# Layer 0 starts with v on unscaled, transposed tokens; v is computed ahead of q and k

## The chip, the cores and the metric

The kernel runs on one core of one Trainium2 chip. A core has TensorE (matrix products, PE in the rows), VectorE (DVE), ScalarE (ACT), GpSimd (POOL) and SyncE (SP), which issues most transfers; each takes its instructions strictly in the order of its own queue and meets the others through semaphores. The metric is the device time of one execution in microseconds (us); the median of three runs of the kernel before is 469.36 (469.34 to 469.58).

## The reference

Two layers of a decoder trunk on 256 tokens of 1024 channels, in float32. What matters here is the front of a layer, and which parts read which:

```
h = rms_norm(x, ln_w)                  # x * rsqrt(mean(x*x) + eps) * ln_w, per token
proj = h @ w_in                        # 1024 x 6672
q, k, v, g_attn, z, xbc, dt_raw = split(proj)
q, k = rms_norm per head (8 heads of 128) of q, k
attn = causal attention with ALiBi (q, k, v) * silu(g_attn)     # 256 tokens: one block
xbc  = silu(causal depthwise conv of width 4 (xbc)); xs, B, C = split(xbc)
dt   = softplus(dt_raw + dt_bias)
y    = SSD scan (xs, dt, a_log, B, C, d_skip) * silu(z), grouped rms_norm
x    = x + concat(attn, y) @ w_out
```

The norm's factor of a token is one number per row, so `(x * ln_w) @ w_v` times that factor, row by row, is the same v.

## The kernel before, in words

Every large product is made of float32r parts: an operand is split into a high part (a cast) and a low part (the operand less its high part), and three products, high-high, low-high and high-low, are added in PSUM. Weights come as a stream of pieces of two k tiles (128 x 2 x 512 numbers for most chunks, 128 x 2 x 348 or 344 for v): `load` (L72) issues the transfer on SyncE into one of four raw buffers, and `pump` (L82) casts the high part on ScalarE (L92) and subtracts for the low part (L94) on VectorE, on GpSimd for pieces 0 and 4. Eight split pieces are held at most, and `free` gives one back after its last product. The chunks go in the order of `CHUNKS` (L34): q0, k0, v0 to v2 (the last holds dt's columns too), q1, k1, and on.

`mm_tokens` (L196) makes q, k, v and the output, tokens on PSUM's partitions, for one half `t` of the 256 tokens over all pieces of a chunk: 24 products for 8 k tiles. q0 and k0 are made for the first 128 tokens and then for the others, while all their eight pieces are held. `mm_pair` (L216) makes x, B, C, g and z with channels on the partitions.

The tokens are loaded with tokens on the partitions. `pre_norm` (L238) normalizes 128 of them: ScalarE's sums of squares, a small "me" on VectorE (L243), the power of -1/2 on GpSimd (L169), the scaling into `hn`, eight transposes on TensorE into `tp`, the product with ln_w on VectorE into `hw`, a cast on ScalarE into `hT` and a subtract on VectorE into `lT`. At the start this runs for the first half ahead of the first product; the second half's runs a little later, its transposes among the products. Ten products of ones (`warm`, L149) stand first on TensorE.

The order on each engine is partly the order of the program, where `manual_schedule` says so (ScalarE, VectorE and TensorE at the start, TensorE at the end of a layer), and otherwise made by a scheduler when the kernel is built. Work behind a product (norms, attention heads, the scan) is written as generators that are resumed some pieces later: `tick` counts pieces, and a `yield n` asks for n more.

Of the kernel before, what the change touches and what calls it, by code (L numbers as in the profile page):

```python
# [9 lines left out]
F32 = mybir.dt.float32  # L10
# [5 lines left out]
P = 128  # L16
# [10 lines left out]
# columns of the per-partition parameters of a layer  # L27
# [21 lines left out]
class Weights:  # L49
    """The stream of weight pieces: loaded ahead, split into two float32r parts."""  # L50

    def __init__(self, nc, raw_pool, wh_pool, wl_pool, w):
# [3 lines left out]
        off = 0  # L56
# [57 lines left out]
def hybrid_kernel(ctx: ExitStack, tc: tile.TileContext, x, par, w, out):  # L114
# [60 lines left out]
    # Work that follows a product is traced a few pieces of weights later, so that the  # L175
    # tensor engine does not wait for it.
# [19 lines left out]
    def mm_tokens(L, name, t, lh, ll, ps, start, stop, last, cols=None):  # L196
# [3 lines left out]
        ts = slice(t * P, (t + 1) * P)  # L200
        cs = slice(*(cols or (0, wd)))
        for s in range(kt // KS):
            ws.pump()
            wh, wl = ws.parts[i0 + s]
            for kk in range(KS):
                kl = k0 % KT + s * KS + kk
                first = start and s == 0 and kk == 0
                final = stop and s * KS + kk == kt - 1
                pe.matmul(ps[:, cs], lh[:, kl, ts], wh[:, kk, cs], start=first, stop=False)  # L209
                pe.matmul(ps[:, cs], ll[:, kl, ts], wh[:, kk, cs], start=False, stop=False)  # L210
                pe.matmul(ps[:, cs], lh[:, kl, ts], wl[:, kk, cs], start=False, stop=final)  # L211
# [26 lines left out]
    def pre_norm(L, t, hT, lT, ms, wait, first=False):  # L238
        """RMS-norm of 128 tokens, split and with the channels on the partitions."""
# [26 lines left out]
        if first:  # L266
            yield 0
# [68 lines left out]
    def decay(L, dtr, dt, dth, ac, nac, cb):  # L336
        """dt = softplus, cumulative sums of dt * exp(a_log): per token and as rows for all."""
# [39 lines left out]
    def conv(L, ps, pr, dst):  # L377
        """Causal convolution and 2 * silu of the channel tiles 2 * pr, 2 * pr + 1."""
# [30 lines left out]
    def ssd_quarter(L, pr, x2, dth, ac, nac, cb, cm, dsh):  # L409
        """Decayed C B products and y of the heads 4 * pr .. 4 * pr + 3."""  # L410
# [83 lines left out]
    for t in range(2):  # L494
        msum[t] = small.tile([P, 2], F32, tag="ms", name=f"ms{t}")
    for j in range(2):
        square_sum(0, j, msum[0])
    for L in range(NL):
        pc = L * NPAR
        if L == 0:  # L500
            hT = keep.tile([P, KT, S], F32R, tag="hT", name=f"hT{L}")
            lT = keep.tile([P, KT, S], F32R, tag="lT", name=f"lT{L}")
            with tc.manual_schedule(engines={mybir.EngineType.Activation, mybir.EngineType.DVE,
                                             mybir.EngineType.PE}):
                start = pre_norm(L, 0, hT, lT, msum[0], 0, True)
                next(start)
                next(start)
                ws.pump(1)
                next(start, None)
                ws.pump(2)  # L510
            ws.pump(4)
            for j in range(2):
                square_sum(1, j, msum[1])
        resume(pre_norm(L, 1, hT, lT, msum[1], 7))

# [1 line left out]
        qT = keep.tile([P, NH, S], F32, tag="qT", name=f"qT{L}")  # L517
        kT = keep.tile([P, NH, S], F32, tag="kT", name=f"kT{L}")
        v_sb = keep.tile([P, 2, D], F32, tag="v", name=f"v{L}")
        aT = keep.tile([P, NH, S], F32, tag="aT", name=f"aT{L}")  # L520
# [7 lines left out]
        def qk(nm, c, t):  # L528
            ps = ps_p.tile([P, 512], F32, tag="ps_p", name=f"{nm}{c}{t}")
            mm_tokens(L, f"{nm}{c}", t, hT, lT, ps, True, True, t == 1)  # L530
            if nm == "q":
                resume(qk_post(L, ps, c, t, qT, C_QN, 1.0, P * EPS))
            else:
                resume(qk_post(L, ps, c, t, kT, C_KN, 1.0 / P, EPS))

        for t in range(2):
            qk("q", 0, t)
            qk("k", 0, t)
# [149 lines left out]
```

## Time and profile before

| | |
|---|---|
| median of three runs | 469.36 us |
| profiled execution, first to last instruction | 467.3 us (its time outside this span isn't recorded) |
| TensorE, VectorE, ScalarE, GpSimd busy | 458.6, 342.4, 278.3, 28.6 us |
| bytes read | 76.8 MB, 167 GB/s over the span |
| granted clock of TensorE, mean | 0.992 |

Times of rows count from the span's first instruction. A product's row is longer than its distance from the next one, since products are pipelined; distances of starts, or the chain of waits, give what one costs in a row.

### The profile page before, as it was taken

What the parts mean: (1) busy time and instruction counts of PE and PEld (TensorE: products, weight loads), DVE (VectorE), ACT (ScalarE), POOL (GpSimd) and SP (SyncE); (2) the same over time, 40 slices, a digit from 0 to 9 for tenths busy, and PEclk for the clock granted to TensorE, in tenths of its full rate; (3) what the DMA queues carried; (4) which work ended last, traced back from release to release, by engine and by line L of the source; (5) the groups of instructions that cost most, each with busy time, mean ns of one, the idle gap of its engine ahead of it and who ended that gap; (6) DMA issues with size and microseconds to landing.
All of it is one profiled execution on the core that took longest, in us unless ns stands there. A gap on an engine that the chain in (4) does not pass through costs nothing.

```text
span 467.3 us, 7748 instructions
## 1 busy us (share of the span) xinstructions
PE 458.6 (98%) x2912; PEld 409.1 (88%) x2912; DVE 342.4 (73%) x621; ACT 278.3 (60%) x563; POOL 28.6 (6%) x31
## 2 busy tenths in 40 slices
PE   5999999999999999999999999999999999999996
PEld 5789987899999898888788899879999989988885
DVE  5765577778999897787385557866899989876721
ACT  6667565987745853446365575678776655555400
POOL 3211001100000000100001100110000000010000
PEclk9799999999999999999999999999999999999999
DMA  7566775832536234536360768574443444434401
GB/s 282 200 193 178 243 271 182 320 131 93 189 130 211 89 118 166 180 129 225 96 194 19 216 212 286 187 299 149 163 156 116 150 165 137 146 103 158 135 24 67
DMA packets 25781, 78.38 MB, mean 168 GB/s; under 512 B 2544, under 2 KB 9104, under 8 KB 25232
## 3 DMA queue, kind: packets, MB, share of 16 engines
q1 hardware_dynamic: 25744, 77.89, 49.3%
q8 instruction: 23, 0.38, 0.3%
q14 instruction: 14, 0.11, 0.1%
HBM read 76.80 MB, written 1.08 MB: 167 GB/s over the span
## 4 chain that ended last, share of the span: by engine, by line
PE 96%; DMA 1%; DVE 1%; ACT 1%; SPq 0%; issue 0%; POOL 0%; DVEq 0%
PE o L210 6%; PE o L209 6%; PE o L211 6%; PE xb L227 5%; PE xb L228 5%; PE xb L229 5%; PE q L210 4%; PE z L229 3%; PE q L211 3%; PE z L228 3%; PE q L209 3%; PE z L227 3%; PE v L209 3%; PE v L211 3%; PE v L210 3%; PE g L228 3%
## 5 line engine op out<-in xcount | busy, mean ns | idle before, releaser
L94 DVE TENSOR_TENSOR wl<-raw,wh 128x1024 fp32r<-128x1024 f32 (+2 forms) x142 | 163.4, 1168 | 44.8 <-ACT wh L92 32.8
L92 ACT CAST wh<-raw 128x1024 fp32r<-128x1024 f32 (+2 forms) x144 | 143.0, 1003 | 63.4 <-PE o L210 21.4
L229 PE MATMUL xb<-hT,wl 128*128 128x256 f32 x192 | 54.8, 285 | 0.0
L228 PE MATMUL xb<-lT,wh 128*128 128x256 f32 x192 | 54.6, 285 | 0.0
L227 PE MATMUL xb<-hT,wh 128*128 128x256 f32 x192 | 54.5, 284 | 0.0
L228 PE MATMUL g<-lT,wh 128*128 128x256 f32 x128 | 36.5, 285 | 0.0
L228 PEld LDWEIGHTS xb<-lT,wh 128*128 128x128 f32 x192 | 36.2, 189 | 0.2
L227 PEld LDWEIGHTS xb<-hT,wh 128*128 128x128 f32 x192 | 36.2, 189 | 0.2
L229 PE MATMUL z<-hT,wl 128*128 128x256 f32 x128 | 36.4, 284 | 0.0
L229 PEld LDWEIGHTS xb<-hT,wl 128*128 128x128 f32 x192 | 36.2, 189 | 0.1
L227 PE MATMUL z<-hT,wh 128*128 128x256 f32 x128 | 36.3, 283 | 0.0
L229 PE MATMUL g<-hT,wl 128*128 128x256 f32 x128 | 36.2, 283 | 0.0
L228 PE MATMUL z<-lT,wh 128*128 128x256 f32 x128 | 36.2, 283 | 0.0
L227 PE MATMUL g<-hT,wh 128*128 128x256 f32 x128 | 36.0, 281 | 0.0
L393 DVE SCALAR_TENSOR_TENSOR cv<-rw,par_sb,cv 128x256 f32<-128x256 f32 x72 | 32.2, 483 | 4.0 <-ACT cv L390 4.0
L209 PE MATMUL v<-wh,hT 128*128 128x348 f32 (+1 forms) x96 | 30.9, 322 | 0.0
L210 PE MATMUL v<-wh,lT 128*128 128x348 f32 (+1 forms) x96 | 30.9, 322 | 0.0
L211 PE MATMUL v<-wl,hT 128*128 128x348 f32 (+1 forms) x96 | 30.8, 321 | 0.0
L209 PE MATMUL q<-wh,hT 128*128 128x512 f32 x64 | 27.2, 425 | 1.3 <-ACT hT L271 1.3
L210 PE MATMUL q<-wh,lT 128*128 128x512 f32 x64 | 26.6, 416 | 1.8 <-DVE lT L274 1.8
L211 PE MATMUL q<-wl,hT 128*128 128x512 f32 x64 | 26.3, 411 | 0.0
L209 PE MATMUL k<-wh,hT 128*128 128x512 f32 x64 | 25.7, 401 | 0.0
(164 smaller groups left out, 1092.3 us busy)
## 6 DMA issues: line engine op xcount, KB each, us to landing
raw<-in_w_dram SPq DMA_DIRECT2D x120, 512.0 KB, 4.3
raw<-in_w_dram SPq DMA_DIRECT2D x16, 348.0 KB, 3.9
cb<-cd SPq DMA_DIRECT2D x4, 1024.0 KB, 5.3
raw<-in_w_dram SPq DMA_DIRECT2D x8, 344.0 KB, 4.3
out_dram<-x SPq DMA_DIRECT2D x3, 256.0 KB, 2.1
x<-in_x_dram SPq DMA_DIRECT2D x2, 256.0 KB, 2.8
x<-in_x_dram SPq DMA_DIRECT2D x1, 512.0 KB, 6.8
out_dram<-x SPq DMA_DIRECT2D x2, 128.0 KB, 1.8
```

Of the source, the lines that this page charges most:

```text
L92: nc.scalar.copy(h[:, :, :wd], src)
L94: sub.tensor_tensor(lo[:, :, :wd], src, h[:, :, :wd].bitcast(F32), ALU.subtract)
L209: pe.matmul(ps[:, cs], lh[:, kl, ts], wh[:, kk, cs], start=first, stop=False)
L210: pe.matmul(ps[:, cs], ll[:, kl, ts], wh[:, kk, cs], start=False, stop=False)
L211: pe.matmul(ps[:, cs], lh[:, kl, ts], wl[:, kk, cs], start=False, stop=final)
L227: pe.matmul(o, wh[:, kk, cs], lh[:, k, :], start=(k == 0 and c == 0), stop=False)
L228: pe.matmul(o, wh[:, kk, cs], ll[:, k, :], start=False, stop=False)
L229: pe.matmul(o, wl[:, kk, cs], lh[:, k, :], start=False, stop=(k == KT - 1 and c == 1))
L393: dve.scalar_tensor_tensor(cv[:, c, :], rw[:, c, k:k + S], cw(k), cv[:, c, :], ALU.mult, ALU.add)
```

## The change

The host lays a transposed copy of x (128 partitions x 8 k tiles x 256 tokens) in front of the weights. It is loaded in four pieces of two k tiles, each ahead of a weight piece, into `xT`; the parameters are loaded from ScalarE's queue, and the row-laid x, in two halves, behind these. `CHUNKS` now begins with v0, v1, v2.

In layer 0, `first_tokens` multiplies a piece of `xT` by ln_w and splits it, without the norm, into `hr` (two casts with a scale on ScalarE) and `lr` (VectorE); v and dt are made of these, and the norm's factor `rs0` is applied when v leaves PSUM on ScalarE and when dt is read. `first_scale` makes `rs0` of the row-laid x. `first_norm` brings the factors to all partitions by two products of ones with a diagonal, multiplies `xT` by them and splits it into `hT` and `lT` for everything after v. The 16 transposes of layer 0 are gone. In layer 1 the norm is as before.

`mm_tokens` takes a list of halves and works each piece for all of them. q and k are made for both halves piece by piece, after v; v0 and v1 of layer 1 are made for the first half of the tokens and then for the second, v2 and all v of layer 0 for both halves piece by piece. The first four attention heads are due at 5, 9, 13 and 17 pieces instead of 1, 5, 9 and 13, counted from after k0.

```diff
-CHUNKS = [(n, 0, 8, 512) for n in ("q0", "k0")]
-CHUNKS += [("v%d" % i, 0, 8, V_W[i]) for i in range(3)]
-CHUNKS += [(n, 0, 8, 512) for n in ("q1", "k1", "x2", "x0", "x1", "g0", "g1", "z0", "z1")]
+CHUNKS = [("v%d" % i, 0, 8, V_W[i]) for i in range(3)]
+CHUNKS += [(n, 0, 8, 512) for n in ("q0", "k0", "q1", "k1", "x2", "x0", "x1", "g0", "g1", "z0", "z1")]
...
-    nc.sync.dma_start(x_sb[0][:, :512], x[0:P, :512])
-    nc.sync.dma_start(x_sb[0][:, 512:], x[0:P, 512:])
     par_sb = const.tile([P, NL * NPAR], F32, name="par_sb")
-    ws.load(0)
-    nc.sync.dma_start(par_sb, par)
-    ws.load(1)
-    nc.sync.dma_start(x_sb[1], x[P:2 * P, :])
+    nc.scalar.dma_start(par_sb, par)
+    xT = keep.tile([P, KT, S], F32, tag="aT", name="xT")
+    xsrc = w[0:NX].rearrange("(p k n) -> p k n", p=P, k=KT)
+    for s in range(KT // KS):
+        ks = slice(s * KS, (s + 1) * KS)
+        nc.sync.dma_start(xT[:, ks, :], xsrc[:, ks, :])
+        ws.load(s)
+    for t in range(2):
+        nc.sync.dma_start(x_sb[t], x[t * P:(t + 1) * P, :])
...
+            for t, ps in zip(ts, pss):
+                tl = slice(t * P, (t + 1) * P)
+                for kk in range(KS):
...
+    def first_tokens(s, hr, lr):
+        ks = slice(s * KS, (s + 1) * KS)
+        for k in range(s * KS, (s + 1) * KS):
+            act.activation(hr[:, k, :], xT[:, k, :], AF.Copy, scale=par_sb[:, C_LN + k:C_LN + k + 1])
+        dve.tensor_tensor(xT[:, ks, :], xT[:, ks, :],
+                          par_sb[:, C_LN + s * KS:C_LN + (s + 1) * KS].unsqueeze(2)
+                          .to_broadcast([P, KS, S]), ALU.mult)
+        dve.tensor_tensor(lr[:, ks, :], xT[:, ks, :], hr[:, ks, :].bitcast(F32), ALU.subtract)
+
+    def first_scale(rs):
+        for t in range(2):
+            ms = small.tile([P, 2], F32, tag="ms", name=f"ms{t}")
+            for j in range(2):
+                square_sum(t, j, ms)
+            me = small.tile([P, 1], F32, tag="me", name="me")
+            dve.scalar_tensor_tensor(me, ms[:, 0:1], EPS, ms[:, 1:2], ALU.add, ALU.add)
+            rpow(rs[:, t:t + 1], me)
+
+    def first_norm(rs, hT, lT):
+        dg = tmp.tile([P, S], F32, tag="sr", name="dg0", bufs=1)
+        for t in range(2):
+            tl = slice(t * P, (t + 1) * P)
+            dve.tensor_scalar(dg[:, tl], ident, rs[:, t:t + 1], None, ALU.mult)
+        yield 2
+        rg = bank("rg0")
+        for t in range(2):
+            tl = slice(t * P, (t + 1) * P)
+            pe.matmul(rg[:, tl], ones, dg[:, tl], start=True, stop=True)
+        for half in range(2):
+            ks = slice(half * 4, half * 4 + 4)
+            dve.tensor_tensor(xT[:, ks, :], xT[:, ks, :],
+                              rg[:, 0:S].unsqueeze(1).to_broadcast([P, 4, S]), ALU.mult)
+            split(hT[:, ks, :], lT[:, ks, :], xT[:, ks, :])
...
+            with tc.manual_schedule(engines={mybir.EngineType.Activation, mybir.EngineType.DVE}):
+                for s in range(KT // KS):
+                    first_tokens(s, hv, lv)
+                    ws.pump(s + 1)
+            rs0 = small.tile([P, 2], F32, tag="rs0", name="rs0", bufs=1)
+            first_scale(rs0)
+        else:
+            hv, lv = hT, lT
+            resume(pre_norm(L, 1, hT, lT, msum[1], 7))
...
+            if L == 0:
+                act.activation(v_sb[:, t, c0:c0 + n], ps[:, :n], AF.Copy, scale=rs0[:, t:t + 1])
...
+        for cs, ts in (((0,), (0, 1)), ((1,), (0, 1)), ((2,), (0, 1))) if L == 0 else (
+                ((0, 1), (0,)), ((0, 1), (1,)), ((2,), (0, 1))):
...
+        qk("q", 0)
+        qk("k", 0)
         for h in range(4):
-            resume(attn_head(h, qT, kT, v_sb, aT, 1 + 4 * h))
+            resume(attn_head(h, qT, kT, v_sb, aT, 5 + 4 * h))
...
-    ws, ps = [], []
+    ws, ps = [f["x"].reshape(S, KT, P).transpose(2, 1, 0).reshape(-1)], []
```

The first rows of ScalarE's queue, with the semaphore that each waits for (DMAHW and a number: a transfer). Before, where `junk` is a sum of squares:

```order
L279 ACT_TABLE_LOAD
L279 ACTIVATE junk,ms_121<-x_84 128x512 [waits DMAHW0_49]
L279 ACTIVATE junk,ms_121<-x_84 128x512 [waits DMAHW1_49,DVE_49,Pool_49]
L252 ACTIVATE hn<-x_84,rs 128x512 [waits Pool_49]
L92 CAST wh_156<-raw_89 128x1024 [waits DMAHW2_49]
L356 ACTIVATE ea<-par_sb 128x16 [waits DMAHW3_49]
L271 CAST hT_127<-hw 128x4x128 [waits DVE_49] x2
L92 CAST wh_166<-raw_92 128x1024 [waits DMAHW4_49]
```

And after, where DMAHW0 is the parameters' transfer, DMAHW1 the first piece of `xT` and DMAHW2 the first weight piece:

```order
L136 DMA par_sb<-in_par_dram 128x236
L281 ACT_TABLE_LOAD [waits DMAHW1_49]
L281 ACTIVATE hr<-xT,par_sb 128x256 [waits DMAHW0_49]
L281 ACTIVATE hr<-xT,par_sb 128x256
L394 ACTIVATE ea<-par_sb 128x16
L92 CAST wh_139<-raw_90 128x2x348 [waits DMAHW2_49]
L281 ACTIVATE hr<-xT,par_sb 128x256 [waits DMAHW3_49]
L281 ACTIVATE hr<-xT,par_sb 128x256
L92 CAST wh_149<-raw_93 128x2x348 [waits DMAHW4_49]
```

The squares, the scaling and the casts of normalized tokens are no longer ahead of the weight pieces; two casts of unscaled tokens stand ahead of each of the first four, and the table load now carries a wait.

GpSimd's queue at the start, before, where `rs` is the power of -1/2 and `wl` the low part of pieces 0 and 4:

```order
L153 IOTA io 128x512
L169 TENSOR_TENSOR rs<-me,mhalf 128x1 [waits DVE_49]
L94 TENSOR_TENSOR wl_157<-raw_89,wh_156 128x1024 [waits DMAHW2_49,Activation_49]
L169 TENSOR_TENSOR rs<-me,mhalf 128x1 [waits DVE_49]
L94 TENSOR_TENSOR wl_209<-raw_164,wh_208 128x1024 [waits DMAHW0_49,Activation_49]
```

After:

```order
L156 IOTA io 128x512
L94 TENSOR_TENSOR wl_140<-raw_90,wh_139 128x2x348 [waits DMAHW2_49,Activation_49]
L172 TENSOR_TENSOR rs_174<-me,mhalf 128x1 [waits DVE_49] x2
L94 TENSOR_TENSOR wl_204<-raw_147,wh_203 128x2x348 [waits DMAHW3_49,Activation_49]
L172 TENSOR_TENSOR rr<-se,mhalf 128x4 [waits DVE_49] x4
```

Both powers have moved behind the first low part and ahead of the second.

TensorE where layer 1 goes from the first half of the tokens to the second, before (`hT` and `lT` are the split tokens, `wh` and `wl` the split weights):

```order
L260 MATMUL tp<-ident,hn 128x128 [waits DVE_49,PE_49]
L260 MATMUL tp<-ident,hn 128x128 x3
L260 MATMUL tp<-ident,hn 128x128 [waits PE_49,Activation_49]
L260 MATMUL tp<-ident,hn 128x128 x3
L211 MATMUL k_2739<-wl_2700,hT_2577 128x512
L209 MATMUL k_2739<-wh_2699,hT_2577 128x512
L210 MATMUL k_2739<-wh_2699,lT_2578 128x512
L211 MATMUL k_2739<-wl_2700,hT_2577 128x512
L300 MATMUL qtp<-ident,qn 128x128 [waits DVE_49]
L300 MATMUL qtp<-ident,qn 128x128 x3
L209 MATMUL q_2800<-wh_2510,hT_2577 128x512 [waits Activation_49]
```

After:

```order
L263 MATMUL tp<-ident,hn 128x128 [waits DVE_49,PE_49]
L263 MATMUL tp<-ident,hn 128x128 x3
L263 MATMUL tp<-ident,hn 128x128 [waits PE_49,Activation_49]
L263 MATMUL tp<-ident,hn 128x128 x3
L213 MATMUL v_2716<-wh_2655,lT_2569 128x348
L214 MATMUL v_2716<-wl_2656,hT_2568 128x348
L212 MATMUL v_2716<-wh_2687,hT_2568 128x348
L213 MATMUL v_2716<-wh_2687,lT_2569 128x348
L214 MATMUL v_2716<-wl_2688,hT_2568 128x348
...
L212 MATMUL v_2760<-wh_2501,hT_2568 128x348 [waits Activation_49]
L212 MATMUL v_2804<-wh_2631,hT_2568 128x348
L213 MATMUL v_2760<-wh_2501,lT_2569 128x348 [waits DVE_49]
```

The second half's transposes stood behind 44 products of 512 columns and four ahead of the half's own; they now stand behind 40 products of 348 columns and eight ahead (three more products of the same piece stand where lines are left out).

## Rows read from the trace of the kernel before

**Rows 1.** The page, busy time of each engine (us, share, instructions).

```profile
PE 458.6 (98%) x2912; PEld 409.1 (88%) x2912; DVE 342.4 (73%) x621; ACT 278.3 (60%) x563; POOL 28.6 (6%) x31
```

**Rows 2.** Waits by engine: who waited for whom, us, times, longest.

```profile
ACT wh L92 <- PE o L210: 21.4, 15, 5.9
...
PE q L210 <- DVE lT L274: 1.8, 1, 1.8
```

**Rows 3.** Chain of waits to 20 us: start, us, what.

```profile
1.65 5.38 DMA raw<-in_w_dram
...
8.83 2.27 DVE lT L274
...
11.13 0.80 PE q L210
...
12.36 0.43 PE q L209
...
16.86 0.87 PE tp L260 x8
17.73 0.24 PE q L211
```

**Rows 4.** Stretches: busy us by engine, granted clock, transfer share, GB/s.

```profile
2.50:3.00 0.50, 0.50 (x4) 0.50 (x4) 0.30 (x1) 0.00 (x0) 0.00 (x0) 1.00 1.01 356
9.00:10.00 1.00, 0.34 (x1) 0.03 (x1) 1.00 (x1) 1.00 (x2) 1.00 (x1) 0.83 1.01 414
16.00:17.00 1.00, 1.00 (x6) 0.81 (x5) 0.00 (x0) 0.17 (x1) 0.75 (x1) 0.75 0.78 266
```

**Rows 5.** Timeline to 9 us: start, us, engine, instruction, idle before.

```profile
0.73 1.28 ACT L279 ACT_TABLE_LOAD   x1 [0.73 <-PEq L673]
...
3.35 0.63 ACT L279 ACTIVATE junk<-x 128x512 f32<-128x512 f32 x1 [1.34 <-DMA x<-in_x_dram]
...
8.18 2.35 POOL L94 TENSOR_TENSOR wl<-raw,wh 128x1024 fp32r<-128x1024 f32 x1 [2.32 <-ACT wh L92]
```

**Rows 6.** Tile lT to 13 us: shortest, median, longest ns; first, last start.

```profile
L274 DVE TENSOR_TENSOR lT<-hw,hT x2: 679/1466/2254, 8.8 to 11.0; 128x512 fp32r<-128x512 f32 x2
```

**Rows 7.** Groups by form: busy us, mean ns; idle before.

```profile
L94 DVE TENSOR_TENSOR wl<-raw,wh 128x696 fp32r<-128x696 f32 x16 | 14.0, 880 | 5.8 <-ACT wh L92 4.9 <-PE q L211 0.9
...
L92 ACT CAST wh<-raw 128x696 fp32r<-128x696 f32 x16 | 12.4, 785 | 6.8 <-DMA raw<-in_w_dram 4.3 <-PE k L210 1.9 <-PE q L210 0.4
...
L263 DVE TENSOR_TENSOR hw<-tp,par_sb 128x512 f32<-128x512 f32 x8 | 5.2, 685 | 2.3 <-PE tp L260 2.3
```

**Rows 8.** Timeline, VectorE at the second norm.

```profile
12.74 0.15 DVE L243 SCALAR_TENSOR_TENSOR me<-ms 128x1 f32<-128x1 f32 x1
13.56 0.49 DVE L250 TENSOR_SCALAR hn<-x,rs 128x512 f32<-128x512 f32 x1 [0.68 <-POOL rs L169]
```

**Rows 9.** Timeline, TensorE where v begins.

```profile
37.37 0.32 PE L209 MATMUL v<-wh,hT 128*128 128x348 f32 x1
37.53 0.32 PE L210 MATMUL v<-wh,lT 128*128 128x348 f32 x1
```

**Rows 10.** Stretches, as rows 4.

```profile
3.50:4.50 1.00, 1.00 (x7) 1.00 (x6) 0.00 (x0) 0.78 (x3) 0.00 (x0) 1.00 0.71 182
22.00:30.00 8.00, 8.00 (x36) 6.43 (x35) 6.25 (x9) 4.34 (x12) 1.02 (x1) 1.00 0.85 249
```

**Rows 11.** Issues of transfers at 3.0 to 3.4 us: KB, us to landing.

```profile
x<-in_x_dram SPq DMA_DIRECT2D x1, 512.0 KB, 6.8
```

**Rows 12.** Timeline about the start of layer 1.

```profile
239.16 0.40 PE L209 MATMUL q<-wh,hT 128*128 128x512 f32 x1
...
243.65 0.72 ACT L252 ACTIVATE hn<-x,rs 128x512 f32<-128x512 f32 x1 [2.19 <-POOL rs L169]
...
249.43 0.27 PE L260 MATMUL tp<-ident,hn 128*128 128x128 f32 x1
...
251.44 0.69 DVE L274 TENSOR_TENSOR lT<-hw,hT 128x512 fp32r<-128x512 f32 x1
```

More of the change, by code (lines that the diff above doesn't have):

```diff
@@ L42 @@
 NB = 8
+NX = P * KT * S
 def w_size():
@@ L55, in __init__ @@
         self.loads, self.subs, self.index = [], [], {}
-        off = 0
+        off = NX
         for l in range(NL):
@@ L194, in drain, with mm_tokens @@
             tick()
-    def mm_tokens(L, name, t, lh, ll, ps, start, stop, last, cols=None):
+    def mm_tokens(L, name, ts, lh, ll, pss, start, stop, last):
         i0 = ws.index[(L, name)]
         k0, kt, wd = next((k, n, c) for nm, k, n, c in CHUNKS if nm == name)
-        ts = slice(t * P, (t + 1) * P)
-        cs = slice(*(cols or (0, wd)))
         for s in range(kt // KS):
@@ L204, in mm_tokens @@
             wh, wl = ws.parts[i0 + s]
[L205 to L211, printed above, removed]
+            for t, ps in zip(ts, pss):
+                tl = slice(t * P, (t + 1) * P)
+                for kk in range(KS):
+                    kl = k0 % KT + s * KS + kk
+                    first = start and s == 0 and kk == 0
+                    final = stop and s * KS + kk == kt - 1
+                    pe.matmul(ps[:, :wd], lh[:, kl, tl], wh[:, kk, :wd], start=first, stop=False)
+                    pe.matmul(ps[:, :wd], ll[:, kl, tl], wh[:, kk, :wd], start=False, stop=False)
+                    pe.matmul(ps[:, :wd], lh[:, kl, tl], wl[:, kk, :wd], start=False, stop=final)
             if last:
@@ L236, in urgent, with pre_norm @@
         return tc.high_priority(offset=URGENT)
-    def pre_norm(L, t, hT, lT, ms, wait, first=False):
+    def pre_norm(L, t, hT, lT, ms, wait):
         xs = x_sb[t]
@@ L493, in hybrid_kernel @@
     msum = [None, None]
[L494 to L497, printed above, removed]
     for L in range(NL):
@@ L502, in hybrid_kernel @@
             lT = keep.tile([P, KT, S], F32R, tag="lT", name=f"lT{L}")
[L503 to L518, printed above, removed]
+            hv = keep.tile([P, KT, S], F32R, tag="qT", name="hr")
+            lv = keep.tile([P, KT, S], F32R, tag="kT", name="lr")
+            with tc.manual_schedule(engines={mybir.EngineType.Activation, mybir.EngineType.DVE}):
[7 more added lines that the diff above has]
+            resume(pre_norm(L, 1, hT, lT, msum[1], 7))
         v_sb = keep.tile([P, 2, D], F32, tag="v", name=f"v{L}")
-        aT = keep.tile([P, NH, S], F32, tag="aT", name=f"aT{L}")
         cb = [keep.tile([P, 8, S], F32, tag=f"cb{g}", name=f"cb{g}_{L}") for g in range(NG)]
@@ L526, in hybrid_kernel @@
         ac, nac = (small.tile([P, NS], F32, tag=n, name=n, bufs=1) for n in ("ac", "nac"))
[L528 to L532, printed above, removed]
-            else:
[L534 to L538, printed above, removed]
@@ L549, in hybrid_kernel, with qk, v_post @@
-        resume(decay(L, dtr, dt, dth, ac, nac, cb))
+        def qk(nm, c):
+            pss = [ps_p.tile([P, 512], F32, tag="ps_p", name=f"{nm}{c}{t}") for t in range(2)]
+            mm_tokens(L, f"{nm}{c}", (0, 1), hT, lT, pss, True, True, True)
+            for t in range(2):
+                if nm == "q":
+                    resume(qk_post(L, pss[t], c, t, qT, C_QN, 1.0, P * EPS))
+                else:
+                    resume(qk_post(L, pss[t], c, t, kT, C_KN, 1.0 / P, EPS))
+        def v_post(c, t, ps):
+            c0 = 348 * c
+            n = min(348, D - c0)
+            b = par_sb[:, pc + C_DTB:pc + C_DTB + NS]
+            if L == 0:
+                act.activation(v_sb[:, t, c0:c0 + n], ps[:, :n], AF.Copy, scale=rs0[:, t:t + 1])
+            else:
+                act.copy(v_sb[:, t, c0:c0 + n], ps[:, :n])
+            if c == 2 and L == 0:
+                dve.scalar_tensor_tensor(dtr[:, t, :], ps[:, n:n + NS], rs0[:, t:t + 1], b,
+                                         ALU.mult, ALU.add)
+            elif c == 2:
+                dve.tensor_tensor(dtr[:, t, :], ps[:, n:n + NS], b, ALU.add)
@@ new lines, in hybrid_kernel @@
+        for cs, ts in (((0,), (0, 1)), ((1,), (0, 1)), ((2,), (0, 1))) if L == 0 else (
+                ((0, 1), (0,)), ((0, 1), (1,)), ((2,), (0, 1))):
+            for c in cs:
+                pss = [ps_p.tile([P, 512], F32, tag="ps_p", name=f"v{c}{t}") for t in ts]
+                mm_tokens(L, f"v{c}", ts, hv, lv, pss, True, True, ts[-1] == 1)
+                if L == 0 and c == 0:
+                    resume(first_norm(rs0, hT, lT))
+                for t, ps in zip(ts, pss):
+                    v_post(c, t, ps)
@@ L555, in hybrid_kernel @@
+        qk("q", 1)
+        qk("k", 1)
         for h in range(4, 8):
```

23 lines of the change are left out of this document (6 added, 17 removed).

## The prediction

> **What bounds the kernel now.** I read the page first: TensorE is busy 458.6 of 467.3 us, 98%, against 342.4 for VectorE and 278.3 for ScalarE [rows 1]. Then the waits: TensorE's longest, 1.8 us, is on one of the first products of q, and none of its few lies behind the start; the weight pieces in turn wait for TensorE to free their buffers (21.4 us in 15 waits at one line alone) [rows 2]. So from about 11 us on the kernel is one queue of products, and a change gains only by starting this queue earlier, by making it shorter, or by keeping the array's clock up. The chain over the first 20 us shows what the start costs: the first weight piece lands at 7.03 us (1.65 + 5.38), its high part and the tokens' high part follow, one subtract on VectorE (lT) takes 2.27 us, and the products run in a row only from 11.13 us [rows 3]. [...]
>
> **Before, in one number.** In TensorE's order 14 products of q stand ahead of the second eight transposes of the tokens, which run from 16.86 to 17.73 us [rows 3]; at 17.73 these and all 16 transposes are done. Fourteen products at 0.233 us are 3.3 us of full-speed work, so it is as if the products had started at 14.4 us and never paused.
>
> **The start after the change.** The new start has no transposes and no norm ahead of the first product, but other things stand in a row.
>
> - First piece of weights. It was third in SyncE's queue with 1.05 MB up to its own end (two halves of x at 0.26, itself 0.52) and landed at 7.03 us. Now one piece of transposed tokens (0.26), 0.36 of its own and the parameters' 0.12, which come over another queue, make 0.74 MB; 0.31 MB less at 356 GB/s [rows 4] is 0.9 us, so it lands at about 6.2 us.
> - ScalarE. In the order shown its table load carries the wait for the first token piece. The first half of x, of the same size, let ScalarE start at 3.35 us; with the parameters' 0.12 MB beside it I take 3.7. The load of 1.28 us ends at 5.0, two scaled casts of 128x256, each under the 0.63 of a 128x512 instruction and put at 0.50, end at 6.0, and the first high part (0.79, with one small instruction ahead) at 7.0 [rows 5, 7].
> - GpSimd makes the first low part. Its 128x1024 form took 2.35 us [rows 5], so 128x696 takes about 1.6. VectorE scales the token piece from 6.0 to 6.7 and subtracts until 7.4. In before the same pairing cost much: while GpSimd ran from 8.18 to 10.53, lT, begun at 8.83, took 2.25 us against 0.68 for its twin [rows 6]. I therefore let each hold the other off: GpSimd works from 7.4 to 9.0, and VectorE goes on at 9.0.
> - VectorE then has three more pieces, each a scaling (0.69), a subtract (0.68) and a low part (0.88) [rows 6, 7]. Of two that don't depend on each other the second starts some 0.08 us before the first ends (11.0 against 8.83 + 2.25) [rows 3, 6], so 2.1 us a piece and 6.3 in all: the fourth piece is ready at 15.3. TensorE needs 12 products of 0.16 us (37.53 - 37.37), 1.9 us, per piece [rows 9] and follows.
> - Norm. It is behind these on VectorE. From a "me" to the instruction that uses its power it took 0.82 us [rows 8], and the diagonal I put at 0.3. GpSimd's order is power, power, low part of the fifth piece: the first power serves a diagonal from 16.1 to 16.4, the second ends at 17.2, and the low part at 18.8. TensorE has by then done 48 products, the two broadcast products and four more, and waits about 1 us.
> - From 18.8 on 92 of the 144 products of v are left, 14.7 us. VectorE's next steps (two scalings and two subtracts of 128x1024, at most twice 0.69 each, and low parts at 0.88) [rows 6, 7] stay ahead of 1.9 us a piece, so v ends at 33.5. Less the 23.0 us that 144 products take, the equivalent start is 10.5 us.
>
> The gain at the start is 14.4 - 10.5 = 3.9 us. Cover that could fail: the row-laid x is behind everything on SyncE. In before x1 was issued in the window from 3.0 to 3.4 and landed 6.8 us later [rows 11], at 9.9, with 2.22 MB up to its end; now 3.64 MB. The 1.42 MB more at 293 to 356 GB/s (249 at a share of 0.85, where pieces of 348 columns were loaded, and 356) [rows 4, 10] makes 13.9 to 14.7 us. With two squares of 0.63 [rows 5] that is in time for the second "me" at 16.4, with 0.4 us to spare or more; each microsecond beyond that is paid in full.
>
> [...]
>
> **The rest.** Layer 1 now begins with v on the first 128 tokens: 48 products of 0.16 us instead of 48 of 0.233. In before the second half's tokens were scaled by 244.4 us (243.65 + 0.72), 5.2 us after the layer's first product at 239.16, its transposes began only at 249.43, and the low part was ready 2.7 us later (251.44 + 0.69) [rows 12]. After, the transposes stand behind 40 products, at 6.4 us, still 1.2 us later than 5.2, and the low part comes at 9.1. TensorE reaches it after 50 products and 0.87 us of transposes, at 8.9. That is a wait of 0.2 us; nearly all the slack is gone, but not more. q and k take both halves of each piece in turn, which frees buffers evenly and adds no instruction. The heads of attention are due in other places; a new wait there has no row in before, where TensorE had none. I bound it by 0 from below and by 1.8, the longest wait TensorE had [rows 2], from above and take 0, since the supply of pieces waits for TensorE and not the reverse.
>
> Sum: 3.9 - 0.2 = 3.7 us. The profiled execution spans 467.3 us; its time outside the span isn't recorded, and the median of 469.36 lies 2.06 above the span. So the span should be 463.6 and the time 465.7 us.
>
> **Rivals.**
>
> - The clock falls as before. In before it fell after a stretch of transposes and a single product, and rose after more than 4 us of unbroken products [rows 3, 4]. If it is at half from 9.7 to 16.5 again, a product takes 0.29 us (0.43 x 348/512): 31 are done at 16.5, and the remaining 17, the broadcasts and four more end at 20.3 instead of 18.8. Then 1.5 us go and the time is 467.2. Against it: real products now run from 7.0 us. [...]
> - VectorE isn't held off, or the loads come sooner. Then VectorE starts its second piece at 8.0, when the casts for it are done, and 1.0 us more is gained: 464.7. For it: lT is a single case. Against it: its size fits GpSimd's end (10.53 + 0.6) closely. If nothing but TensorE bound from 7.0 us on, 462.3 would be the floor.
> - The gain is given back later, at the boundary or among the moved heads, to no change, about 469. For it: the slack at the boundary goes to nearly nothing. Against it: one wait of 1.8 us would not do, two would be needed.
> - Slower: the loads of the start starve the norm. There are 1.05 MB more of them. From 3.5 to 4.5 us the engines moved only 182 GB/s [rows 10]. If that is the rate of small rows, x1 with 3.64 MB lands at 20.0 + 3.6 (the constant that fits x1 in before at 356 GB/s), 8.5 us past 15.1, and the time is 474.2. It decides from 225 GB/s down, where x1 lands at 19.8. Against it: the rows of the token pieces are as long as those of x in before, which moved at 356.
>
> **Chances.** The forecast 0.56 (its own range 465.0 to 466.6), VectorE free or loads sooner 0.18, clock 0.14, no change 0.07, slower 0.05. The first three are all faster by over 0.2% (0.94 us, about what a measurement here can tell from no change): 0.88 faster, 0.07 same, 0.05 slower. The range from 463.6 to 468.0 holds the first three and leaves out the last two and a start better than I can account for.
>
> **What would show it.** The first product of v near 7.0 us; a stretched VectorE instruction while GpSimd makes its first low part; VectorE without a gap from there to the first "me" near 15.3; TensorE waiting about 1 us for GpSimd's second low part; v's last product near 33.5; the clock at 1.00 throughout. It would be wrong if TensorE had waits past 40 us, if x1 landed after 15.1, or if the clock fell with the products running.

## The result: 464.45 us, but not for the forecast's reason

The changed kernel takes 464.45 us (median of 6 runs, 463.00 to 467.34; five of them lie up to 464.67, and why one took 467.34 isn't known) against 469.35 (6 runs, 468.99 to 469.58). The ratio is 0.9902, with a 95% interval from 0.9881 to 0.9922. The forecast was 465.7, with a range from 463.6 to 468.0 (465.0 to 466.6 for its own case). The profiled execution spans 461.9 us and took 463.97.

The time lies in the range. The gain does not lie where it was forecast: of the 5.4 us between the spans, the start holds a little over one. First the page of the changed kernel, busy time by engine (us, share, instructions), to be set beside [rows 1], and the shares of the chain that ended last:

```profile
PE 451.5 (98%) x2900; PEld 403.7 (87%) x2900; DVE 348.0 (75%) x625; ACT 280.3 (61%) x567; POOL 31.6 (7%) x31
...
PE 91%; DMA 3%; DVE 3%; ACT 1%; POOL 1%; issue 0%; SPq 0%; DVEq 0%; POOLq 0%
```

TensorE is busy 7.1 us less although it has the same weight products to make and only 12 instructions fewer. That alone should make a reader suspicious: a start that merely moves to the left leaves the busy time as it is. Now its waits (us in all, times, longest), which answer to [rows 2]:

```profile
PE v L212 <- ACT wh L92: 3.5, 2, 3.2
...
PE tp L263 <- DVE hn L253: 0.8, 1, 0.8
PE v L214 <- POOL wl L94: 0.6, 1, 0.6
PE pp L364 <- DVE sc L359: 0.3, 1, 0.3
PE v L214 <- DVE wl L94: 0.2, 1, 0.2
```

The 3.2 us are the idle time ahead of v's first product. The 0.8 stands at the end of layer 0, ahead of the first half's transposes, where the forecast had nothing. The start itself, in order of time (start, us, engine, instruction, idle before), answers to [rows 5, 6, 8]:

```profile
5.12 1.28 ACT L281 ACT_TABLE_LOAD   x1 [5.12 <-DMA xT<-in_w_dram]
...
6.41 0.91 ACT L281 ACTIVATE hr<-xT,par_sb 128x256 fp32r<-128x256 f32 x2
...
8.14 0.95 PE L212 MATMUL v<-wh,hr 128*128 128x348 f32 x2 [3.23 <-ACT wh L92]
8.17 2.13 POOL L94 TENSOR_TENSOR wl<-raw,wh 128x696 fp32r<-128x696 f32 x1 [6.77 <-ACT wh L92]
...
8.93 1.92 DVE L282 TENSOR_TENSOR xT<-xT,par_sb 128x512 f32<-128x512 f32 x1 [0.16 <-ACT hr L281]
...
16.53 0.15 DVE L294 SCALAR_TENSOR_TENSOR me<-ms 128x1 f32<-128x1 f32 x1
...
18.32 1.69 POOL L94 TENSOR_TENSOR wl<-raw,wh 128x696 fp32r<-128x696 f32 x1
18.39 1.71 DVE L302 TENSOR_SCALAR dg<-ident,rs 128x128 f32<-128x128 f32 x1 [0.68 <-POOL rs L172]
```

Everything from the first token piece on is 1.1 to 1.4 us later than forecast: the table load begins at 5.1 (3.7), v's first product at 8.14 (7.0), "me" at 16.53 (15.3), GpSimd's second low part ends at 20.0 (18.8). The granted clock, in stretches of 1 us as in [rows 4] (it stands behind the five engines' busy times):

```profile
7.00:8.00 1.00, 0.00 (x0) 0.00 (x0) 0.65 (x1) 1.00 (x4) 0.00 (x0) 0.67 1.05 372
8.00:9.00 1.00, 0.86 (x3) 0.68 (x4) 0.81 (x3) 1.00 (x4) 0.83 (x1) 0.50 1.05 381
...
13.00:14.00 1.00, 1.00 (x6) 1.00 (x4) 1.00 (x2) 0.96 (x3) 0.00 (x0) 0.50 1.01 322
14.00:15.00 1.00, 1.00 (x7) 1.00 (x7) 1.00 (x2) 0.98 (x4) 0.00 (x0) 0.91 1.01 323
```

So the granted clock was at half (0.50) from about 7.3 to 14.2 us. Before, it was at half from 9.7 to 16.5: 0.83 in the microsecond from 9 and 0.75 in that from 16 [rows 4], 0.50 in all between. v's last product:

```profile
35.85 0.32 PE L214 MATMUL v<-wl,hr 128*128 128x344 f32 x1
```

It ends at 36.17 us; less 23.0 us of products that is an equivalent start of 13.1 us, against 14.4 before. 1.3 us are gained, not 3.9. (In a second profile of the same kernel, e3 below, v ends at 35.65, which makes 1.8: a loss of 0.5 us at 25.2, for the high part of a piece, is absent there.)

The rest shows when one compares what should be equal. Here is TensorE's timeline of before in two stretches in which nothing but weight products runs, first and last of them: z with 256 columns, 74 steps from product to product, and the output projection with 512 columns, 71 steps.

```profile
164.93 0.28 PE L228 MATMUL z<-lT,wh 128*128 128x256 f32 x1
...
173.68 0.28 PE L227 MATMUL z<-hT,wh 128*128 128x256 f32 x1
...
215.51 0.39 PE L209 MATMUL o<-wh,sh 128*128 128x512 f32 x1
...
232.07 0.40 PE L211 MATMUL o<-wl,sh 128*128 128x512 f32 x1
```

In the changed kernel the corresponding z stretch is longer, 158 steps:

```profile
168.23 0.28 PE L232 MATMUL z<-hT,wl 128*128 128x256 f32 x1
...
186.14 0.28 PE L231 MATMUL z<-lT,wh 128*128 128x256 f32 x1
```

A step takes 8.75/74 = 118.2 ns before and 17.91/158 = 113.4 ns after, at the same shape, in the same order of the three parts, with the granted clock at 1.00 in both. Over all weight products that directly follow one of the same width past 40 us, the mean step is 118.3 ns before and 114.8 after for 256 columns (1274 and 1228 steps), 233.3 and 229.2 ns for 512 columns (626 and 712). The few steps above 150 and 280 ns are left out, here and below (32 and 22 in before). The change touches none of this, except that its tiles lie elsewhere in SBUF.

### The profile page after: what moved, and what is told of

It is laid out like the page before. It is cut to its first block, busy times and chain, and to the rows that moved or that the text cites. A ratio compares the mean times of both kernels' runs of the same rounds, so it can differ in the third digit from the quotient of the medians.

```text
span 461.9 us, 7752 instructions
## 1 busy us (share of the span) xinstructions
PE 451.5 (98%) x2900; PEld 403.7 (87%) x2900; DVE 348.0 (75%) x625; ACT 280.3 (61%) x567; POOL 31.6 (7%) x31
## 4 chain that ended last, share of the span: by engine, by line
PE 91%; DMA 3%; DVE 3%; ACT 1%; POOL 1%; issue 0%; SPq 0%; DVEq 0%; POOLq 0%
PE o L212 6%; PE o L214 6%; PE o L213 6%; PE xb L231 4%; PE xb L232 4%; PE xb L230 4%; PE z L231 3%; PE z L232 3%; PE k L212 3%; PE g L230 3%; PE g L232 3%; PE q L213 3%; PE k L213 3%; PE g L231 3%; PE z L230 3%; PE k L214 3%
## 5 line engine op out<-in xcount | busy, mean ns | idle before, releaser
L230 PE MATMUL xb<-hT,wh 128*128 128x256 f32 x192 | 56.0, 292 | 0.0
L172 POOL TENSOR_TENSOR rr<-se,mhalf 128x4 f32<-128x4 f32 x16 | 18.0, 1123 | 126.5 <-DVE se L328 90.7
L212 PE MATMUL o<-wh,ah 128*128 128x512 f32 x64 | 25.5, 398 | 0.0
L213 PE MATMUL k<-wh,lT 128*128 128x512 f32 x64 | 25.4, 397 | 0.0
L214 PE MATMUL k<-wl,hT 128*128 128x512 f32 x64 | 25.3, 395 | 0.0
L213 PE MATMUL o<-wh,al 128*128 128x512 f32 x64 | 25.2, 394 | 0.0
L212 PE MATMUL o<-wh,sh 128*128 128x512 f32 x64 | 25.2, 394 | 0.0
```

What stands on the lines that cost most here:

```text
L172: pool.tensor_tensor(o, i, mhalf[:, :n], ALU.pow)
L212: pe.matmul(ps[:, :wd], lh[:, kl, tl], wh[:, kk, :wd], start=first, stop=False)
L213: pe.matmul(ps[:, :wd], ll[:, kl, tl], wh[:, kk, :wd], start=False, stop=False)
L214: pe.matmul(ps[:, :wd], lh[:, kl, tl], wl[:, kk, :wd], start=False, stop=final)
L230: pe.matmul(o, wh[:, kk, cs], lh[:, k, :], start=(k == 0 and c == 0), stop=False)
```

## Experiments

### Where the tiles lie: e1, e2, e3

In the built programs hT begins at byte 29792 of a partition before and at 37984 after, the first weight buffer wh at 162688 and 162720. Token tiles are 8192 bytes apart and weight buffers 4096, so one distance modulo 256 stands for all pairs: wh less hT is 32 before and 64 after. The extra 32 bytes come from the small tiles in between, among them the new `rs0`. One unused tile undoes or imitates this without touching an instruction. The same edit in the kernel before (e1) and in the changed one (e2):

```diff
+    pad = ctx.enter_context(tc.tile_pool(name="pad", bufs=1)).tile([P, 8], F32, name="pad")
     raw_pool = ctx.enter_context(tc.tile_pool(name="raw_pool", bufs=RAWB))
```

Expected of e1:

> The kernel before, with 32 unused bytes per partition set aside in front of the weight buffers, so that raw, wh and wl stand 32 bytes further on, where the changed kernel has them; no instruction differs. In the profile of before a 512-column product starts 233.3 ns after the one ahead of it and a 256-column one 118.4 ns; in the profile of the changed kernel 229.2 ns and 113.3 or 117.8 ns. Theory A (the addresses set the spacing): 512 columns at about 229 ns and many of the 256-column products at 113 ns, 469.4 falls to about 464 to 466 us. Theory B (the new order of the products, both token halves piece by piece, sets it): spacing and time as before, 469.0 to 469.6 us. Theory C (the spacing is a matter of the single execution): times spread over some us, as those of the changed kernel do (463.0 to 467.3).

Expected of e2:

> The changed kernel with 32 unused bytes per partition in front of the weight buffers, so that they stand at a multiple of 64 bytes again, as in before; no instruction differs. Theory A (addresses): 512-column products at about 233 ns and 256-column ones at about 118 ns, time about 4 us longer, 468 us. Theory B (order of the products): 464.5 us as the changed kernel. Theory C (chance): no fixed difference, spread of some us.

e3 is the changed kernel once more, with no edit. Expected:

> The changed kernel itself once more, as the measure for the others of this call and for a second profile. Theories A and B: spacing 229.2 ns for 512 columns, 113.3 and 117.8 ns for 256 columns, as in the first profile; 463 to 465 us. Theory C: another spacing in this profile, 233 ns perhaps, and a time that follows it, up to 467 us.

Measured: e1 took 462.74 us (462.70 to 463.35; ratio to before 0.9865, interval 0.985 to 0.988). e2 470.14 (469.51 to 470.42; ratio 1.0016, 1.0007 to 1.0024). e3 464.26 (463.63 to 464.74). Theory A holds, with effects even larger than expected. The two stretches of before, in e1's timeline, with the same number of steps:

```profile
162.97 0.28 PE L229 MATMUL z<-lT,wh 128*128 128x256 f32 x1
...
171.38 0.28 PE L228 MATMUL z<-hT,wh 128*128 128x256 f32 x1
...
212.28 0.40 PE L210 MATMUL o<-wh,sh 128*128 128x512 f32 x1
...
228.55 0.40 PE L212 MATMUL o<-wl,sh 128*128 128x512 f32 x1
```

A step takes 8.41/74 = 113.6 and 16.27/71 = 229.2 ns; in before, 118.2 and 16.56/71 = 233.2. And in e2 the z stretch of the changed kernel, 158 steps:

```profile
169.79 0.28 PE L233 MATMUL z<-hT,wl 128*128 128x256 f32 x1
...
188.32 0.28 PE L232 MATMUL z<-lT,wh 128*128 128x256 f32 x1
```

That is 117.3 ns again. The mean steps past 40 us account for the time: in e1 1274 steps of 256 columns at 115.3 instead of 118.3 ns are 3.8 us, 626 of 512 at 229.6 instead of 233.3 are 2.3, together 6.1 of the 6.6 us gained. Order (theory B) and chance (theory C) are out: e1 has before's order to the instruction, and e3 repeats the first result.

So, with the tiles at the same distance of 64, the change costs time: 464.26 against 462.74, 1.5 us. (e2 has a third distance, 96, slow as before's 32; there the changed kernel is 0.8 us behind before.) One empty tile without the change gives more than the change did.

### Which distance: e5, e6, e9, e12, e10

e5 moves everything from hT on by 32 bytes; e6 adds e1's tile to that.

```diff
     x_sb = [keep.tile([P, D], F32, tag=f"x{t}", name=f"x{t}") for t in range(2)]
+    gap = keep.tile([P, 8], F32, tag="gap", name="gap")
```

Expected of e5, then of e6:

> The kernel before with 32 unused bytes ahead of the token tiles hT, lT and all that follows: now hT, lT and the gated tiles stand at multiples of 64 bytes and the weight buffers 32 bytes past one. Addresses modulo 64 so far (hT, wh): before 32, 0 and slow (469.4); e1 and the changed kernel 32, 32 and fast (462.7, 464.3); e2 32, 0 and slow (470.1). Theory A1 (the two operands must stand alike modulo 64): 32 bytes apart again, so slow, 469 us. Theory A2 (only the weight buffers count, and they must not stand at a multiple of 64): fast, 462.7 us. Theory A3 (each operand off a multiple of 64 helps by itself): between, 466 us.

> The kernel before with 32 unused bytes ahead of hT and 32 more ahead of the weight buffers: both operands at multiples of 64 bytes. Theory A1 (alike modulo 64): fast, 462.7 us, with 512-column products at 229 ns and 256-column ones at 113 or 118 ns. Theory A2 (weights must not stand at a multiple of 64): slow, 469.4 us. Theory A3 (each by itself): slowest of all, 469 us or more.

e9 and e12 are e1 with `[P, 24]` and `[P, 40]` in place of `[P, 8]`, 96 and 160 bytes. Expected:

> The kernel before with 96 unused bytes in front of the weight buffers. In the runs so far the fast kernels have hT and wh 64 bytes apart modulo 128 (e1: 96 and 32, the changed kernel 96 and 32, e6: 0 and 64), the slow ones 32 apart (before: 96 and 0, e5: 0 and 32). Here both stand at 96 modulo 128. Theory A1 (alike modulo 64 is what counts): fast, 462.7 us, 512-column products 229 ns apart. Rival (64 bytes apart modulo 128 is what counts): slow, 469 us.

> The kernel before with 160 unused bytes in front of the weight buffers. The byte address of wh0 less that of hT was so far, modulo 256: 32 (before, e5), 96 (e2), 128 (e9), all slow, and 64 (e1, e6, the changed kernel), all fast. Here it is 192. Theory F (64 modulo 128 is what counts): fast, 462.7 us as e1, 512-column products 229 ns apart. Rival (64 modulo 256, or some longer period): slow, 469.4 us, 233 ns. If the time lies elsewhere, the rule is not one of distance alone.

e10 is e1 with another such tile between wh and wl:

```diff
+    gap = ctx.enter_context(tc.tile_pool(name="gap", bufs=1)).tile([P, 8], F32, name="gap")
     wl_pool = ctx.enter_context(tc.tile_pool(name="wl_pool", bufs=NB))
```

> e1 (before with all weight buffers 32 bytes on: 462.7 us) with 32 more unused bytes between the high parts wh and the low parts wl: modulo 64 the tokens stand at 32, wh at 32, wl at 0. A third of the products reads wl. Theory M1 (a product pays for its own pair of operands, or for its weights' load beside the product ahead): only every third interval is longer, a third of the 6.6 us comes back, 464.9 us. Theory M2 (once one of them is apart the rhythm is lost for all): 469 us. Theory M3 (the low parts don't count): 462.7 us.

Measured, with the mean steps taken as above:

| kernel | wh less tokens, mod 256 | step, 512 columns | step, 256 columns | median us |
|---|---|---|---|---|
| before | 32 | 233.3 ns | 118.3 ns | 469.35 |
| e5, all moved alike | 32 | 233.2 | 118.3 | 469.36 |
| e1 | 64 | 229.6 | 115.3 | 462.74 |
| e6, all moved | 64 | 229.6 | 115.0 | 463.06 |
| changed kernel, e3 | 64 | 229.2 | 114.8 | 464.26 |
| e2 (changed kernel) | 96 | 233.5 | 117.7 | 470.14 |
| e9 | 128 | 232.4 | 118.8 | 469.50 |
| e12 | 192 | 233.2 | 117.5 | 468.43 |
| e10: wh 64, wl 96 | both | 231.2 | 118.3 | 467.90 |

It is the distance of the two operands that counts, not the place of either: e5 moved all and changed nothing, e6 brought the distance to 64 in another place and was fast. Two of my rules for the distance fell. "Alike modulo 64" passed e5 and e6 and fell with e9 (0 modulo 64, slow). "64 modulo 128" fell with e12 (192). What stands is a list: 64 was fast in three places; 32, 96, 128 and 192 were slow; 0, 160 and 224 weren't run. A longer period than 256 isn't excluded.

e10 came out as none of its theories had it: 5.2 of 6.6 us came back, though only a third of the products reads wl. Its output products from 215 to 228 us, grouped by line (busy time, mean ns of one instruction from its start to its end, idle time), and the same groups in before:

```profile
L212 PE MATMUL o<-wh,sl 128*128 128x512 f32 x19 | 7.5, 396 | 0.0
L211 PE MATMUL o<-wh,sh 128*128 128x512 f32 x19 | 7.4, 389 | 0.0
L213 PE MATMUL o<-wl,sh 128*128 128x512 f32 x18 | 7.1, 395 | 0.0
```

```profile
L211 PE MATMUL o<-wl,sh 128*128 128x512 f32 x18 | 7.1, 395 | 0.0
L209 PE MATMUL o<-wh,sh 128*128 128x512 f32 x18 | 7.1, 395 | 0.0
L210 PE MATMUL o<-wh,sl 128*128 128x512 f32 x18 | 7.1, 395 | 0.0
```

The products go in the order wh,sh, wh,sl, wl,sh. In e10 the first is 6 to 7 ns shorter than the other two, in before all three are equal. The distances of starts say the same over the whole run: with 512 columns the step from wh,sh to wh,sl is 227.2 ns in the mean, the step to the product with wl 233.1 and the one behind it 233.4; in before these are 233.5, 233.2 and 233.1, in e1 229.0, 229.3 and 230.6. So two of three steps became slow, and with 256 columns all three (118.3, 118.6 and 118.0 ns). Since the slow steps of 512 columns go by product, writes of other engines into these buffers are an unlikely cause; that is argued, not shown.

Theory M1 fell with both of its readings, a product that pays for its own two operands and a load for the next product that gets in the way of the present one: either gives one slow step in three. The measurement decides that distance matters; by which mechanism stays open.

### The start: e4, e8

```diff
-WARM = 10
+WARM = 18
```

Expected of e4:

> The changed kernel with 18 warm-up products in place of 10: at 0.37 us each they end at about 7.8 us in place of 4.9, just ahead of the first v product (8.1). If the idle time from 4.9 to 8.1 us is what brought the granted clock down from 7.3 to 14.1 us, it stays at 1.00 and the start gains until the low parts of pieces 3 and 4 (ready at 16.6 and 20.0 us) stop the engine: 93 products of v are left at 20.0, so that v ends at about 34.7 in place of 36.2 us and the kernel takes 1.0 to 1.5 us less, about 463.2. If the clock falls for another reason (products that wait for their pieces), nothing changes: 464.5.

Measured: 462.53 us (462.31 to 462.80), 1.7 below e3. The clock stayed at 1.00, and v ended at 35.33 instead of 36.17 (35.65 in e3). TensorE's waits now:

```profile
PE rg L307 <- DVE dg L302: 1.1, 1, 1.1
...
PE v L214 <- POOL wl L94: 0.9, 1, 0.9
PE v L212 <- ACT wh L92: 0.8, 1, 0.8
```

The idle time from the end of the warm-up (4.91 us; 5.29 in e3) to v's first product was what brought the clock down: with all but 0.8 us of it filled, and nothing else changed, it did not fall. With the products at full speed TensorE waits longer on GpSimd's account: 0.9 us, instead of 0.6, for the low part of the first piece, and 1.1 up to 19.9 us for a diagonal that VectorE did not finish while GpSimd worked (1.69 us beside a low part that took GpSimd from 18.09 to 19.76, against 0.29 for the other diagonal). (The forecast had its wait of 1 us at this place for the fifth piece's low part itself.)

So the gain is not where it was expected. Of the 2.0 us that e4 leads e3 by at 14.9 us, 0.3 are left at the end of v. Another 1.2 come between 80 and 92 us, among the first attention heads, where e3 waits twice for VectorE (0.3 us each, for `qn` and `sc`) and e4 does not; the rest of that isn't settled.

e8 takes GpSimd out as well:

```diff
-ON_POOL = (0, 4)
+ON_POOL = ()
```

> The changed kernel with 18 warm-up products and with the low parts of pieces 0 and 4 on VectorE in place of GpSimd. With 18 warm-ups alone (e4, 462.5) VectorE's scaling of the tokens took 1.92 us beside GpSimd's first low part in place of 0.69, and TensorE waited 1.05 us up to 19.9 us for the low part of piece 4, which GpSimd began 18.1 us only, behind its two power steps. Theory E (GpSimd's two low parts are the cost): VectorE makes wl0 0.9 us more but is not held off (1.2 us less), has wl3 at about 15.9 and wl4 at about 16.8 us; 98 products are left then, v ends at about 32 us in place of 35.2, the kernel takes about 3 us less than e4: 459.5. Rival (VectorE is the start's bound anyway, or the loads are): within 0.5 us of e4, 462 to 463.

Measured: 459.51 us (459.46 to 459.66; ratio to before 0.9791, interval 0.9777 to 0.9804), as expected of theory E to the tenth, which is in part luck: v ends 2.4 us earlier than in e4 (counted as below) and not the 3.2 that the theory had, and the rest comes behind it. Two rows of VectorE and TensorE's waits in e8:

```profile
9.20 0.68 DVE L282 TENSOR_TENSOR xT<-xT,par_sb 128x512 f32<-128x512 f32 x1
...
16.93 0.88 DVE L94 TENSOR_TENSOR wl<-raw,wh 128x696 fp32r<-128x696 f32 x1 [0.24 <-ACT wh L92]
```

```profile
PE v L212 <- ACT wh L92: 1.0, 1, 1.0
PE tp L263 <- DVE hn L253: 0.8, 1, 0.8
PE v L214 <- DVE wl L94: 0.2, 1, 0.2
```

The scaling that took 1.92 us beside GpSimd takes 0.68, and v is delayed 0.2 us in all once it runs. v ends at 33.81, with four q products (0.9 us) already among it, so the equivalent start is 33.8 - 0.9 - 23.0 = 9.9 us. This is the start that the forecast was about, and it is worth 4.5 us against 14.4. Against e1, which has the same distance of tiles, e8 gains 3.2 us: that is what this change and the two edits are worth together. How much of it is the change's own isn't shown: no run gives the kernel before the same two edits, though its clock falls too (0.50 from 10 to 16 us) and its GpSimd makes the same low parts.

### The moved attention heads: e7, e11

In the order of TensorE's instructions other products break the runs of weight products 84 times in the changed kernel and 63 times in before. e7 brings the breaks down to 65:

```diff
             for t, ps in zip(ts, pss):
+                if t == 1 and name[0] in "qk":
+                    tick()
                 tl = slice(t * P, (t + 1) * P)
...
-            resume(attn_head(h, qT, kT, v_sb, aT, 5 + 4 * h))
+            resume(attn_head(h, qT, kT, v_sb, aT, 5 + 3 * h))
```

> The changed kernel with the clock of the postponed work counted by token half in q and k again (two steps a piece), heads 0 to 3 of the attention at 5, 8, 11 and 14 steps: their products stand among q1 and k1 again in place of among x2. In the order of TensorE's instructions the runs of weight products are broken 65 times by other products, against 84 times in the changed kernel and 63 in before. Theory D (the breaks are what the change pays: at equal addresses the changed kernel gains 1.9 us up to the end of v, q and k's own time, and loses 2.9 us later, 0.14 us for each of the 21 more breaks): 19 breaks fewer, 2.6 us less, 461.7 us. Rival (the other products take their time wherever they stand; what is lost is the stall at the layer's end and the like): 464.0 to 464.5 us.

e11 puts e4's, e8's and e7's edits together:

> The changed kernel with the three edits that gained by themselves: 18 warm-up products, the low parts of pieces 0 and 4 on VectorE (both: e8, 459.5 us) and the steps of postponed work counted by token half in q and k (e7: 463.0 against 464.3 us of the changed kernel in the call before). If the gains add up, as parts of different stages should: 458.2 us. If what e7 gained is the start's (its v ended 0.3 us earlier, its clock fell in some runs only): 459.2 to 459.5.

Measured: e7 463.00 us (462.64 to 463.76), half of what theory D expected. e11 459.53 (459.48 to 460.06), nothing beyond e8 with breaks down from 84 to 66. So the breaks aren't the price, and theory D fell. What e7 removed is in layer 0, between the first x2 and the first output product. In the changed kernel and in e7:

```profile
84.11 0.37 PE L230 MATMUL xb<-hT,wh 128*128 128x256 f32 x1
...
188.94 0.40 PE L212 MATMUL o<-wh,ah 128*128 128x512 f32 x1
```

```profile
84.11 0.28 PE L232 MATMUL xb<-hT,wh 128*128 128x256 f32 x1
...
187.57 0.39 PE L214 MATMUL o<-wh,ah 128*128 128x512 f32 x1
```

104.8 us (105.1 in e3) against 103.5. In e4, whose products stand in the order of the changed kernel, the stretch from the same x2 product is 104.2 (83.27 to 187.51); in e8 it is 103.5 too (81.28 to 184.81), but there the products stand in another order. So an earlier start takes some 0.6 us off this stretch, in rows that waited for VectorE, and the rest of the 1.3 isn't settled. The expectation of e11 has e7's clock fall in some runs only; that isn't shown. e7's profile lists 1.00 at 12 us, but its products of v start 0.29 us apart there, as those of the changed kernel do at half clock.

## Why the prediction was right in its number and wrong in its reason

- **The place of the tiles** was no term of the sum. It is worth 6.6 us in before (e1) and 5.9 in the changed kernel (e2 less e3), more than all terms together. The step that failed first is the sentence that a change gains *only* by starting the queue earlier, shortening it, or keeping the clock up: it took the step of 0.233 us (233.3 ns in the table) as given. At equal distance the change costs 1.5 us where a gain of 3.7 was forecast, so that the time came into the range by luck. It lies nearest to the rival with 464.7 us, whose condition did not come either: VectorE was held off (1.92 us for a scaling that takes 0.69 without GpSimd), and the loads came later (the first token piece at 5.04 us).
- **The start**, 3.9 us forecast, 1.3 measured (1.8 in e3). Three terms failed. The first pieces: the first token piece landed at 5.04 us, so that the table load began 1.4 us late, and GpSimd needed 2.13 instead of 1.6 us, as if it had waited for the subtract on VectorE that ran from 8.07 to 8.76 us; together 1.2 us on every later step. The clock: it fell at 7.3 us, 2.4 earlier than in [rows 3, 4], and came back at 14.2. That products from 7.0 us on would keep it up was an estimate of mine, and it failed: with products running from 8.14 us the clock was at 0.50 until 14.2. I looked at these products and not at the gap of 3.23 us between the warm-up and them; with 0.8 us left of this gap the clock stayed at 1.00 (e4). The rival of the falling clock priced it at 1.5 us, with 0.29 us for a product of 348 columns at half clock, which is what one took (12.26 to 12.55 us); e4 measured 1.7 in all, at other places. Behind 20 us, VectorE and ScalarE were to stay ahead of TensorE: it lost 0.4 us at 22.7 for a low part that stood behind the scaling of 128x1024 (1.22 us), and 0.5 at 25.2 for a high part.
- **GpSimd against VectorE** was rightly counted as a loss (1.92 us beside GpSimd against 0.69 without it, as [rows 6] had it for `lT`; what the two contend for isn't shown) and gave the largest one: 3.0 us from e4 to e8, where the forecast counted 1.0 for it and about 1 of waiting at piece 4. It missed the second collision, where the diagonal's TENSOR_SCALAR took 1.71 instead of 0.29 us.
- **x1's landing** was right: it landed at 14.31 us, within the forecast 13.9 to 14.7, and its squares began at 14.39 without a wait. The rival of starved loads did not come.
- **The rest**, 0.2 us forecast. The wait that this names came, and at its place: TensorE had made 50 products of v when it came to the second half's low part, 9.16 us after layer 1's first product (9.1 forecast). The step to this product is 0.45 us instead of 0.16:

```profile
245.38 0.42 PE L213 MATMUL v<-wh,lT 128*128 128x348 f32 x1
```

Two losses were not in the sum. The prediction says that none of TensorE's waits in before lies behind the start; one does, 0.2 us ahead of the first half's transposes for layer 1, and in the changed kernel it is 0.8. The transposes in before and in the changed kernel:

```profile
232.65 1.06 PE L260 MATMUL tp<-ident,hn 128*128 128x128 f32 x8 [0.18 <-DVE hn L250]
```

```profile
229.79 1.09 PE L263 MATMUL tp<-ident,hn 128*128 128x128 f32 x8 [0.77 <-DVE hn L253]
```

VectorE there, in the changed kernel and in e1:

```profile
228.45 0.88 DVE L94 TENSOR_TENSOR wl<-raw,wh 128x696 fp32r<-128x696 f32 x1 [0.50 <-ACT wh L92]
229.25 0.48 DVE L253 TENSOR_SCALAR hn<-x,rs 128x512 f32<-128x512 f32 x1
```

```profile
228.54 0.48 DVE L251 TENSOR_SCALAR hn<-x,rs 128x512 f32<-128x512 f32 x1 [0.67 <-POOL rs L170]
```

The low part of a v piece now stands ahead of the scaling that the transposes need. The other loss is that of 1.3 us in the stretch from x2 to the output of layer 0. Starts of layer 1 in e1, in the changed kernel and in e8 show what is left of the start at equal distance:

```profile
235.59 0.39 PE L210 MATMUL q<-wh,hT 128*128 128x512 f32 x1
```

```profile
236.22 0.48 PE L212 MATMUL v<-wh,hT 128*128 128x348 f32 x2
```

```profile
232.05 0.32 PE L212 MATMUL v<-wh,hT 128*128 128x348 f32 x1
```

Of 1.3 us gained at the start, 0.5 went at the boundary and 1.3 in the stretch behind x2: the changed kernel begins layer 1 0.6 us later than e1, which is what these rows say. e8 begins it 3.5 earlier. From there to the end both take 0.5 us more than e1, 0.3 of it at the product at 245.38 (241.20 in e8). The rival "given back later" was nearer to the truth than its 0.07, hidden by the tiles.

Of the signs that the forecast named, VectorE came as said: stretched beside GpSimd's first low part, and without a gap from there to "me". The others did not: no wait for GpSimd's second low part, v's last product near 36 us, the clock at half. And TensorE waited past 40 us, which was to show the forecast wrong: 0.3 us for `sc` in layer 0, and the 0.8 above.

## What to carry to other kernels

When an edit moves the time, compare steps that it should not have touched: products in a row, same shape, same clock. If they differ, look where the tiles lie, and move one of them by an empty tile of 32 bytes (6.6 us in e1) before believing any story about order; try several sizes, since no simple rule held here. Let the warm-up reach to the first real product (in e4 the clock stayed at 1.00 where it had been at 0.50, and 1.7 us were gained), and don't let GpSimd subtract beside the VectorE instructions that bound the start (1.92 us for one that takes 0.68 without it; 3.0 us from e4 to e8).

## What the runs showed of the hardware

- The step between equal float32r products differed with the byte distance of their two SBUF operands: 113 to 115 ns (e1, e6 and the changed kernel) against 117 to 119 (before, e2, e5, e9, e12) for 256 columns, 229 against 232 to 234 for 512 (64 modulo 256 against 32, 96, 128 and 192). This is 1.4% of the kernel (e1).
- In the changed kernel a VectorE TENSOR_SCALAR of 128x128 (`dg`, from `ident` and the one column `rs`) took 1.71 us beside a GpSimd subtract that began 0.07 us ahead of it, and 0.29 without one.
- In the changed kernel TensorE was idle from 4.91 to 8.14 us; its granted clock was 0.50 from about 7.3 to 14.2, with products running from 8.14. With all but 0.8 us of the gap filled (e4) it stayed at 1.00.
